# mLSTM with both parts summed in PSUM from scaled queries, and 24 modulation vectors of layer 0 on the matrix engine

## The chip, the cores and the metric

The kernel runs on one core of a Trainium2 chip. The metric is the device time of one execution in microseconds (us), here the median of three runs. PE is the matrix engine, DVE the vector engine, ACT the scalar engine, POOL the GpSimd engine, SP the queue that issues the loads and stores.

## What is computed

One inference step of two layers over 1152 tokens (1024 latent tokens and 128 context tokens) of width 1024. Each layer modulates its input with six vectors of 1024 made from `c` (latent tokens) and `c_ctx` (context tokens), projects it to three groups of heads (latent attention, mLSTM, HGRN2), joins them by an output projection, and ends in a gated feed-forward part. What the change touches is the modulation and the mLSTM:

```python
mod = (jax.nn.silu(cvec) @ lp['w_mod'] + lp['b_mod'])[:, None, :]
sh1, sc1, g1, sh2, sc2, g2 = jnp.split(mod, 6, axis=-1)
...
def step(carry, inp):                      # mlstm_scan, one chunk, one direction
    ...
    mt = jnp.maximum(a, Dm.max(-1))
    ws = jnp.exp(a - mt)
    qk = jnp.einsum('bhtd,bhsd->bhts', qc, kc) * jnp.exp(Dm - mt[..., None])
    num = ws[..., None] * jnp.einsum('bhtd,bhde->bhte', qc, C) + jnp.einsum('bhts,bhse->bhte', qk, vc)
    den = ws * jnp.einsum('bhtd,bhd->bht', qc, n) + qk.sum(-1)
    h = num / jnp.maximum(jnp.abs(den), jnp.exp(-mt))[..., None]
...
h = hf + flip(hb)                          # mlstm_mixer: both directions, then per head
mu = h.mean(-1, keepdims=True)
var = jnp.mean(jnp.square(h - mu), -1, keepdims=True)
h = (h - mu) * lax.rsqrt(var + EPS)
```

## The kernel before

The two layers run one after the other, each in four phases: A (all input projections, HGRN2, the preparation of attention, mLSTM), B (attention), C (output projection, layer norm), D (feed-forward). Instructions are not left in the order of the source: a list scheduler places each on its engine as soon as its inputs and its buffers allow, the one that stands first in the source going first. Each engine then runs its own list strictly in order, and SP issues nearly all loads and stores, also in order. Matmuls with an accurate product are written as three (L155, L156, L157: high by high, low by high, high by low part); those of the mLSTM are plain float32.

**Modulation.** The 48 vectors of a layer's `w_mod`, 128 results each, are 512 KB apiece. At the very start of the kernel vectors 8 to 15 of layer 0 are made on PE (L251 in `start`, eight matmuls of 128x2 each) and vectors 0 to 7 on DVE. The other vectors of layer 0 up to 39 are made by `start_mod` on DVE, where `mod_gemv` does two products with a sum over 1024 columns per vector (L213), each with a read of the accumulator, and `mod_bias` adds the bias (L220) for eight vectors at once. Vectors 16 to 23 run beside the `gi` projection and the preparation of attention in phase A; behind them a small transposition on PE (`gsave`, L225) writes them out. Vectors 24 to 39 run in the mLSTM loop of layer 0, two after each chunk. Layer 1's vectors are made elsewhere and are not touched.

**mLSTM.** `mlstm` is called at the end of phase A of each layer and runs over nine chunks of 128 tokens; the ninth holds the context tokens and has no earlier state. Per chunk, SP loads a stabiliser table `nb` (broadcast, 512 KB) and the queries `qc`. PE makes the four query-key products (L832); POOL masks (L834), ACT takes eight exponentials of 128x128 (L837), DVE multiplies the two (L841, four times 256 columns). Then, for each direction, PE makes the part from the state (L847, two matmuls of 130 columns) in one PSUM bank; DVE scales it by `ws` into SBUF (L848); PE makes the part inside the chunk (L852, four matmuls of 65 columns) in another bank; DVE adds it (L855, or L857 in the ninth chunk). Denominators are three small operations on DVE (L860, L861, L862). The division (L865, twice) runs on POOL in layer 0 and on DVE in layer 1, POOL adds the directions (L866), DVE takes mean and variance (L869, L871, L873), POOL the power (L874), and two passes subtract the mean and scale (L876, on POOL in layer 0, on DVE in layer 1). The exponentials `ws` are made earlier, in `ml_gates`.

Behind the loop in the source stand two spills (`mo`, `gg`: projections with 256 columns in the banks of the ring `r_mm`, three of the eight PSUM banks), and then phase B. The scheduler pulls matmuls of both into the mLSTM's stretch. The first attention scores are L1136, with a row maximum on DVE (L1137) between them; L1182 is the first use of the finished weights.

## Time and profile before

| what | us |
|---|---|
| median of 3 runs | 3642.04 (3641.22 to 3644.99) |
| the profiled execution | 3641.28 |
| its span in the trace | 3639.5 |
| PE busy | 3405.9 |
| DVE busy | 2264.8 |
| layer 0, first L832 to first L1182 (479.6 to 613.7) | 134.1 |
| layer 1, the same (2288.1 to 2393.7) | 105.6 |

The profile gives one execution; every duration comes from it. A busy PE is counted by records, whose ends are modelled; the clock granted to PE is given for a stretch as a share of the full 2.4 GHz, 0.50 being 1.2 GHz. A wait is the idle time of an engine just before an instruction, with the one that released it.

### The profile page before, as it was taken

How to read it: one execution, taken by the hardware profiler on the slowest of the kernel's cores; microseconds unless marked ns; L12 is line 12 of the kernel's file. 1: busy time of each engine (PE TensorE's matmuls, PEld its weight loads, DVE VectorE, ACT ScalarE, POOL GpSimd, SP SyncE). 2: the span in 40 equal slices, each digit the busy share in tenths (PEclk: the TensorE clock that was granted, in tenths of full speed). 3: DMA queues.
4: the chain of work that ended last, by engine and by line, in shares of the span. 5: the costliest groups of instructions: out<-in, count | busy, mean ns of one | idle time of the engine just before them, and what ended most of it. 6: DMA issues, size and time to landing. Idle time of an engine off the chain costs nothing. (4 is left out here: it accounts for less than half of the span.)

```text
span 3639.5 us, 56085 instructions
## 1 busy us (share of the span) xinstructions
PE 3405.9 (94%) x20556; PEld 3034.6 (83%) x20556; DVE 2264.8 (62%) x4492; ACT 1635.7 (45%) x2877; POOL 1988.8 (55%) x1745
## 2 busy tenths in 40 slices
PE   7999987999989999999889989989999999999997
PEld 7998875776779999988689888877767899998875
DVE  6868878555674444487775678765558544443246
ACT  4264564887343333312272636577853433333211
POOL 3455566777665555401453556567863555552176
PEclk9899976999989999999999999789999999999998
DMA  6212153002352222375422021401044322224222
GB/s 244 72 40 43 39 167 100 18 21 81 121 160 85 85 85 85 111 252 179 156 79 62 30 45 34 137 25 25 22 132 139 110 73 73 73 74 139 94 99 80
DMA packets 331272, 335.77 MB, mean 92 GB/s; under 512 B 191458, under 2 KB 270386, under 8 KB 330996
## 3 DMA queue, kind: packets, MB, share of 16 engines
q1 hardware_dynamic: 330996, 332.19, 29.5%
q8 instruction: 161, 2.64, 0.3%
q14 instruction: 115, 0.94, 0.1%
HBM read 263.54 MB, written 68.56 MB: 91 GB/s over the span
## 5 line engine op out<-in xcount | busy, mean ns | idle before, releaser
L151 POOL TENSOR_TENSOR t<-t,t 128x512 fp32r<-128x512 f32 (+3 forms) x318 | 437.8, 1378 | 374.8 <-ACT t L150 374.4
L150 ACT CAST t<-t 128x512 fp32r<-128x512 f32 (+5 forms) x404 | 270.7, 673 | 698.0 <-PE bank L1449 278.7
L1449 PE MATMUL bank<-hhi,t 128*128 128x256 f32 (+1 forms) x2816 | 570.8, 295 | 12.4 <-DVE t L1349 11.5
L155 PE MATMUL bank<-hhi,t 128*128 128x384 f32 (+1 forms) x1220 | 455.1, 378 | 19.2 <-ACT t L150 5.1
L157 PE MATMUL bank<-hhi,t 128*128 128x384 f32 (+1 forms) x1220 | 460.0, 378 | 8.8 <-DVE t L151 8.8
L1449 PEld LDWEIGHTS bank<-hhi,t 128*128 128x128 f32 x2816 | 456.2, 189 | 13.6 <-ACT t L150 12.3
L156 PE MATMUL bank<-hlo,t 128*128 128x384 f32 (+1 forms) x1220 | 460.9, 378 | 4.9 <-POOL hlo L151 4.1
L1187 POOL TENSOR_TENSOR t<-t,t 128x512 fp32r<-128x512 f32 (+1 forms) x304 | 383.3, 1281 | 125.4 <-ACT t L1186 103.0
L1449 PE MATMUL bank<-t,t 128*128 128x320 f32 (+1 forms) x3168 | 434.2, 297 | 2.3 <-DVE t L1507 1.7
L1449 PEld LDWEIGHTS bank<-t,t 128*128 128x128 f32 x3168 | 427.9, 190 | 3.7 <-DVE t L1507 1.9
L1449 PE MATMUL bank<-hlo,t 128*128 128x320 f32 (+1 forms) x1408 | 415.2, 295 | 0.0
L155 PE MATMUL bank<-t,hhi 128*128 128x256 f32 (+3 forms) x1232 | 386.8, 315 | 12.1 <-DVE t L1107 5.4
L156 PE MATMUL bank<-t,hhi 128*128 128x256 f32 (+3 forms) x1232 | 388.0, 315 | 4.3 <-POOL t L146 4.3
L157 PE MATMUL bank<-t,hlo 128*128 128x256 f32 (+3 forms) x1232 | 388.4, 316 | 0.3 <-POOL hlo L151 0.3
L155 PEld LDWEIGHTS bank<-hhi,t 128*128 128x128 f32 x1220 | 237.9, 196 | 57.3 <-ACT t L150 6.7
L1137 DVE TENSOR_REDUCE t<-bank 128x1 f32<-128x384 f32 (+1 forms) x400 | 203.9, 538 | 122.6 <-PE bank L1136 119.5
L157 PEld LDWEIGHTS bank<-hhi,t 128*128 128x128 f32 x1220 | 240.1, 197 | 39.2 <-DVE t L151 12.1
L156 PEld LDWEIGHTS bank<-hlo,t 128*128 128x128 f32 x1220 | 239.6, 196 | 34.7 <-POOL hlo L151 5.1
L1449 PEld LDWEIGHTS bank<-hlo,t 128*128 128x128 f32 x1408 | 265.4, 188 | 0.3 <-issue 0.2
L155 PEld LDWEIGHTS bank<-t,hhi 128*128 128x128 f32 x1232 | 239.8, 195 | 30.2 <-DVE t L1107 5.6
L213 DVE SCALAR_TENSOR_TENSOR t<-t,t 128x1024 bf16<-128x1024 f32 x176 | 239.3, 1359 | 40.6 <-DMA t<-in_w_mod_dram 31.6
L156 PEld LDWEIGHTS bank<-t,hhi 128*128 128x128 f32 x1232 | 240.4, 195 | 20.1 <-POOL t L146 4.7
(355 smaller groups left out, 7329.1 us busy)
## 6 DMA issues: line engine op xcount, KB each, us to landing
t<-in_w_mod_dram SPq DMA_DIRECT2D x96, 512.0 KB
t<-in_w_ffn_in_dram SPq DMA_DIRECT2D x88, 512.0 KB
t<-in_w_ffn_out_dram SPq DMA_DIRECT2D x44, 512.0 KB
t<-in_w_in_dram SPq DMA_DIRECT2D x40, 512.0 KB
shid<-t SPq DMA_DIRECT2D x88, 160.0 KB
sx<-t SPq DMA_DIRECT2D x27, 512.0 KB
t<-sx SPq DMA_DIRECT2D x27, 512.0 KB
shid<-t SPq DMA_DIRECT2D x88, 128.0 KB
```

Of the source, the lines that this page charges most:

```text
L150: self.nc.scalar.copy(hi, src)
L151: (eng or self.nc.gpsimd).tensor_tensor(lo, src, hi.bitcast(F32), op=ALU.subtract)
L155: mm(ps, a[0], b[0], start=first, stop=False)
L156: mm(ps, a[0], b[1], start=False, stop=False)
L157: mm(ps, a[1], b[0], start=False, stop=last)
L213: nc.vector.scalar_tensor_tensor(junk, raw, 1.0, cB[s], op0=ALU.mult, op1=ALU.mult, accum_out=self.modfm[:, l, j, s:s + 1])
L1137: V.tensor_reduce(nm[:, i, b:b + 1] if i < 8 else nm[:, i, 3:4], ps, axis=AX.X, op=ALU.max, negate=True)
L1187: G.tensor_tensor(pl, e, ph.bitcast(F32), op=ALU.subtract)
L1449: mm(ps, a[x][:, k * P:(k + 1) * P], view(y, k, n0, n1), start=first and k == 0 and i == 0, stop=k == 3 and i == 2, skip_group_check=True)
```

## The change

In the mLSTM, the scale `ws` goes to the queries instead of to the product: SP loads the exponents broadcast over partitions (two loads per chunk and eight chunks per layer), ACT takes one Exp of 128x512, POOL multiplies by the queries, and PE's state part (now L862) and inside part (L865) accumulate in one PSUM bank per direction. L848, L855 and L857 are gone. The four products of L841 become two of 512 columns (L856). Denominators and the division (L869 to L875) read PSUM on DVE, in both layers. The last subtraction and scaling become four ACT operations of 128x64 per chunk (L888), with one small operation on DVE for the bias (L886).

The 24 vectors 16 to 39 of layer 0 are made on PE (L292, eight matmuls of 128x2 each, from a transposed packing of `w_mod`), three after each chunk of layer 0's mLSTM, into a PSUM bank of their own. That bank is taken from `r_mm`, which has two banks for the spills there. The preparation of attention has no vectors beside it any more, and `gsave` of vectors 16 to 23 moves into the mLSTM. Three buffers of 512 KB take turns for the loads, where there were two.

```diff
-    def start_mod(self, z, j0, j1):
-        raw = z.ring(2, [P, U])
-        cB, junk = [z([P, D]), z([P, D])], z([P, D], BF16)
-        self.mod_init(cB)
+    def start_mod(self, z, j0, j1, bank):
+        nc = self.nc
+        raw = z.ring(3, [P, U])
 
         def gen():
             for j in range(j0, j1):
-                self.mod_gemv(0, j, cB, raw.next(), junk)
+                w, ps = raw.next(), bank[:, 2 * (j - j0):2 * (j - j0) + 2]
+                nc.sync.dma_start(w, self.ins["w_mod"][0, j])
+                for i in range(KD):
+                    nc.tensor.matmul(ps, w[:, i * P:(i + 1) * P], self.cc[:, i, :], start=(i == 0), stop=(i == KD - 1))
                 if j % 8 == 7:
-                    self.mod_bias(0, j - 7, 8)
+                    g = j - 7
+                    b = self.col(0, "bmod")[:, g:g + 8].unsqueeze(2).to_broadcast([P, 8, 2])
+                    pv = bank[:, 2 * (g - j0):2 * (g - j0) + 16].rearrange("p (j s) -> p j s", s=2)
+                    nc.vector.scalar_tensor_tensor(self.modfm[:, 0, g:g + 8, :], pv, 1.0 if (g // 8) % 3 == 1 else 0.0, b,
+                                                   op0=ALU.add, op1=ALU.add)
...
-                        bg = self.start_mod(Zone(self, c, "gemv"), 16, 24) if l == 0 else iter(())
+                        bg = iter(())
...
-                bg = self.start_mod(zl, 24, 40) if l == 0 else iter(())
+                bg = iter(())
+                if l == 0:
+                    self.r_mm = self.banks(0, 1)
+                    bg = self.start_mod(zl, 16, 40, self.bank[2])
...
-            nc.scalar.activation(ws[:, :, 4 * d:4 * d + 4], nts[:, :, 2 + d, :], AF.Exp)
...
+            if n < 8:
+                wq = rwq.next()
+                for e in range(2):
+                    nc.sync.dma_start(wq[64 * e:64 * e + 64], bass.AP(tensor=sws.tensor, offset=sws.offset + e * T + n * P,
+                                                                      ap=[[0, 64], [4 * T, 2], [2 * T, 2], [1, P]]))
+                nc.scalar.activation(wq, wq, AF.Exp)
+                G.tensor_tensor(wq, wq, qc.unsqueeze(1).to_broadcast([P, 2, 2, P]), op=ALU.mult)
...
-                for d in range(2):
-                    V.tensor_tensor(nbv[:, d, :, e, :], psq[e][:, 0:256].rearrange("p (a t) -> p a t", a=2), nbv[:, d, :, e, :], op=ALU.mult)
-            num = rnum.next()
+                pq = psq[e][:, 0:256].rearrange("p (a t) -> p a t", a=2).unsqueeze(1).to_broadcast([P, 2, 2, P])
+                V.tensor_tensor(nbv[:, :, :, e, :], pq, nbv[:, :, :, e, :], op=ALU.mult)
+            den, pv = rden.next(), []
             for d in range(2):
+                ps = self.r_m.next()
                 if n < 8:
-                    psn = self.r_m.next()
                     for p in range(2):
-                        nc.tensor.matmul(psn[:, p * 130:(p + 1) * 130], qc[:, p, :], Cst[d][:, n, p].rearrange("p e c -> p (e c)"), start=True, stop=True)
-                    V.tensor_tensor(num[:, d], psn[:, 0:260].rearrange("p (h c) -> p h c", h=4),
-                                    ws[:, n, 4 * d:4 * d + 4].unsqueeze(2).to_broadcast([P, 4, 65]), op=ALU.mult)
-                psi = self.r_m.next()
+                        nc.tensor.matmul(ps[:, p * 130:(p + 1) * 130], wq[:, d, p, :], Cst[d][:, n, p].rearrange("p e c -> p (e c)"),
+                                         start=(p == 0), stop=False, skip_group_check=True)
                 for h in range(4):
-                    nc.tensor.matmul(psi[:, h * 65:(h + 1) * 65], nb[:, 4 * d + h, :], vaug[:, n, h, :], start=True, stop=True)
-                pv = psi[:, 0:260].rearrange("p (h c) -> p h c", h=4)
-                if n < 8:
-                    V.tensor_tensor(num[:, d], pv, num[:, d], op=ALU.add)
-                else:
-                    V.tensor_copy(num[:, d], pv)
-            den = rden.next()
-            dv = den.rearrange("p (d h) -> p d h", d=2)
-            V.scalar_tensor_tensor(dv, num[:, :, :, 64], -1.0, num[:, :, :, 64], op0=ALU.mult, op1=ALU.max)
-            V.tensor_tensor(den, den, emt[:, n, :], op=ALU.max)
-            V.reciprocal(den, den)
-            h1 = rh.next()
+                    nc.tensor.matmul(ps[:, h * 65:(h + 1) * 65], nb[:, 4 * d + h, :], vaug[:, n, h, :], start=(n == 8 and h == 0),
+                                     stop=(h == 3), skip_group_check=True)
+                pv.append(ps[:, 0:260].rearrange("p (h c) -> p h c", h=4))
+                dd = den[:, 4 * d:4 * d + 4]
+                V.tensor_tensor(dd, pv[d][:, :, 64], emt[:, n, 4 * d:4 * d + 4], op=ALU.max)
+                V.scalar_tensor_tensor(dd, pv[d][:, :, 64], -1.0, dd, op0=ALU.mult, op1=ALU.max)
+            rd = den[:, 0:8]
+            V.reciprocal(rd, rd)
+            hs = [rh.next() for _ in range(2)]
             for d in range(2):
-                (LG).tensor_tensor(num[:, d, :, 0:64], num[:, d, :, 0:64], den[:, 4 * d:4 * d + 4].unsqueeze(2).to_broadcast([P, 4, 64]), op=ALU.mult)
-            G.tensor_tensor(h1, num[:, 0, :, 0:64], num[:, 1, :, 0:64], op=ALU.add)
+                V.tensor_tensor(hs[d], pv[d][:, :, 0:64], den[:, 4 * d:4 * d + 4].unsqueeze(2).to_broadcast([P, 4, 64]), op=ALU.mult)
+            h1 = hs[0]
+            G.tensor_tensor(h1, h1, hs[1], op=ALU.add)
...
-            for i, op in ((0, ALU.subtract), (1, ALU.mult)):
-                (LG).tensor_tensor(h1, h1, mv[:, :, i:i + 1].to_broadcast([P, 4, 64]), op=op)
+            V.scalar_tensor_tensor(mb, mv[:, :, 0], -1.0, rs, op0=ALU.mult, op1=ALU.mult)
+            for h in range(4):
+                nc.scalar.activation(h1[:, h, :], h1[:, h, :], AF.Identity, bias=mb[:, h:h + 1], scale=mv[:, h, 1:2])
...
-            for _ in range(2):
+            for _ in range(3):
```

How the work stands on PE in the middle of layer 0's mLSTM, before. L832 are query-key products, L847 state parts, L852 inside parts; L155 to L157 belong to a spill:

```order
L832 MATMUL bank_66<-t_4391,t_612 128x128 x2
L157 MATMUL bank_63<-t_131,hlo_77 128x256
L155 MATMUL bank_63<-t_131,hhi_76 128x256
L156 MATMUL bank_63<-t_135,hhi_76 128x256
L157 MATMUL bank_63<-t_131,hlo_77 128x256
L847 MATMUL bank_69<-t_2979,t_4387 128x130 x2
L847 MATMUL bank_68<-t_2983,t_4387 128x130
L852 MATMUL bank_70<-t_608,t_4371 128x65 x3
L847 MATMUL bank_68<-t_2983,t_4387 128x130
L832 MATMUL bank_67<-t_4391,t_612 128x128 x2
L155 MATMUL bank_64<-t_147,hhi_76 128x256
```

Between the mLSTM's matmuls stand runs of 256-column matmuls; no vector is on PE. After, at about the same chunk (L847 is now the query-key product, L862 the state part, L865 the inside part, L292 a vector, `x8` its eight matmuls, `bank_65` the vectors' bank):

```order
L292 MATMUL bank_65<-cc_84,t_4284 128x2
L292 MATMUL bank_65<-cc_84,t_4288 128x2 x8
L292 MATMUL bank_65<-cc_84,t_4292 128x2 x8
L847 MATMUL bank_66<-t_4320,t_608 128x128
L847 MATMUL bank_67<-t_4320,t_608 128x128
L847 MATMUL bank_66<-t_4320,t_608 128x128
L847 MATMUL bank_67<-t_4320,t_608 128x128
L862 MATMUL bank_69<-t_2918,t_4332 128x130 x2
L862 MATMUL bank_70<-t_2922,t_4332 128x130 x2
L292 MATMUL bank_65<-cc_84,t_4284 128x2 x7
L865 MATMUL bank_69<-t_604,t_4300 128x65 x4
L865 MATMUL bank_70<-t_604,t_4300 128x65 x4
```

Vectors, three per chunk, stand between the inside parts of one chunk and the products of the next, and again ahead of the inside parts; in this place there is no matmul of a spill. The first vector stands behind most of the spills' matmuls and the last some 110 rows later; between them are nine matmuls of 256 and six of 384 columns.

On DVE, in the middle of layer 0's mLSTM, before (L151 splits operands of attention):

```order
L848 TENSOR_TENSOR t_4399<-bank_69,t_2807 128x260
L151 TENSOR_TENSOR hlo_77<-t_5692,hhi_76 128x384 x2
L213 SCALAR_TENSOR_TENSOR t_4361,modfm_80<-t_4349,t_4357 128x1024
L151 TENSOR_TENSOR hlo_77<-t_5692,hhi_76 128x384
L855 TENSOR_TENSOR t_4395<-bank_68,t_4395 128x260
L862 RECIPROCAL t_4407<-t_4407 128x8
L873 TENSOR_SCALAR t_4439<-t_4439 128x4
L855 TENSOR_TENSOR t_4399<-bank_70,t_4399 128x260
L213 SCALAR_TENSOR_TENSOR t_4361,modfm_80<-t_4345,t_4353 128x1024
L860 SCALAR_TENSOR_TENSOR t_4411<-t_4395 128x8
L841 TENSOR_TENSOR t_4375<-bank_66,t_4375 128x2x128 x2
```

After, at the same chunk's place:

```order
L856 TENSOR_TENSOR t_4300<-bank_66,t_4300 128x4x128
L856 TENSOR_TENSOR t_4300<-bank_67,t_4300 128x4x128
L869 TENSOR_TENSOR t_4340<-bank_69,t_2744 128x4
L870 SCALAR_TENSOR_TENSOR t_4340<-bank_69,t_4340 128x4
L869 TENSOR_TENSOR t_4340<-bank_70,t_2744 128x4
L870 SCALAR_TENSOR_TENSOR t_4340<-bank_70,t_4340 128x4
L297 SCALAR_TENSOR_TENSOR modfm_80<-bank_65,cols_78 128x16
L872 RECIPROCAL t_4340<-t_4340 128x8
L875 TENSOR_TENSOR t_4352<-bank_69,t_4340 128x256
L875 TENSOR_TENSOR t_4356<-bank_70,t_4340 128x256
```

The L213 are gone from between the mLSTM's operations, and one L297 per eight vectors adds the bias out of the vectors' bank.

On PE in phase A, before, inside the input projections of 176 columns:

```order
L157 MATMUL bank_64<-t_131,hlo_77 128x176
L155 MATMUL bank_64<-t_131,hhi_76 128x176
L156 MATMUL bank_64<-t_135,hhi_76 128x176
L225 MATMUL bank_68<-ident_71,modfm_80 16x128
L157 MATMUL bank_64<-t_131,hlo_77 128x176
L155 MATMUL bank_65<-t_147,hhi_76 128x176
```

After, the same transposition (now L226) stands in layer 0's mLSTM, behind the first eight vectors:

```order
L862 MATMUL bank_68<-t_2918,t_4324 128x130 x2
L862 MATMUL bank_69<-t_2922,t_4324 128x130 x2
L156 MATMUL bank_64<-t_136,hhi_76 128x256
L157 MATMUL bank_64<-t_132,hlo_77 128x256
L226 MATMUL bank_70<-ident_71,modfm_80 16x128
L292 MATMUL bank_65<-cc_84,t_4292 128x2 x8
L865 MATMUL bank_68<-t_604,t_4308 128x65 x4
```

It moved out of the projections of phase A.

## Rows read from the trace of the kernel before

**Rows 1.** The page, part 1: busy us (share of the span) and count per engine.

```profile
PE 3405.9 (94%) x20556; PEld 3034.6 (83%) x20556; DVE 2264.8 (62%) x4492; ACT 1635.7 (45%) x2877; POOL 1988.8 (55%) x1745
```

**Rows 2.** Windows: us, busy by engine (count), PE clock, DMA share, GB/s.

```profile
479.60:613.70 134.10, 96.33 (x464) 81.07 (x464) 119.84 (x325) 54.82 (x121) 94.86 (x96) 0.68 0.50 157
2288.10:2377.70 89.60, 78.62 (x420) 71.44 (x419) 74.72 (x261) 53.04 (x131) 52.28 (x61) 0.72 0.47 138
2288.10:2393.70 105.60, 88.00 (x443) 77.59 (x443) 89.11 (x286) 59.00 (x140) 55.10 (x65) 0.68 0.41 123
```

**Rows 3.** Lines of DVE, 479.6 to 613.7: busy us, mean ns, idle before, releaser.

```profile
L213 DVE SCALAR_TENSOR_TENSOR t<-t,t 128x1024 bf16<-128x1024 f32 x32 | 44.1, 1377 | 5.7 <-DMA t<-in_w_mod_dram 3.7 <-DMA t<-scr 1.9
...
L213 DVE DVE_READ_ACCUMULATOR t<-t,t 128x1 f32 x32 | 2.5, 77 | 0.0
```

**Rows 4.** Window of phase A, layer 0.

```profile
80.00:140.00 60.00, 49.13 (x349) 47.56 (x348) 59.97 (x122) 23.88 (x31) 31.27 (x26) 0.85 0.29 94
```

**Rows 5.** Lines of DVE, 70 to 140.

```profile
L213 DVE SCALAR_TENSOR_TENSOR t<-t,t 128x1024 bf16<-128x1024 f32 x16 | 20.9, 1309 | 4.6 <-DMA t<-scr 4.6
```

**Rows 6.** Waits of PE, 70 to 150: line, releaser, us, times, longest.

```profile
PE bank L225 <- DVE modfm L220: 4.2, 1, 4.2
```

**Rows 7.** Timeline of PE: start us, us, line, tiles, form, count.

```profile
24.07 3.41 PE L251 MATMUL bank<-t,t 128*128 128x2 f32 x16
27.34 0.67 PE L155 MATMUL bank<-hhi,t 128*128 128x384 f32 x1
...
34.72 1.84 PE L251 MATMUL bank<-t,t 128*128 128x2 f32 x16
36.42 0.42 PE L155 MATMUL bank<-hhi,t 128*128 128x384 f32 x1
```

**Rows 8.** Windows that show the granted clock.

```profile
34.00:37.00 3.00, 3.00 (x25) 3.00 (x24) 0.37 (x3) 0.08 (x1) 1.80 (x1) 1.00 1.02 405
51.00:56.00 5.00, 5.00 (x18) 5.00 (x19) 3.72 (x10) 2.17 (x2) 0.00 (x0) 0.50 0.01 3
510.00:520.00 10.00, 5.76 (x24) 5.05 (x23) 9.94 (x29) 7.45 (x18) 5.93 (x6) 0.50 0.82 260
2310.00:2330.00 20.00, 20.00 (x97) 18.63 (x98) 16.38 (x58) 16.42 (x52) 8.22 (x11) 0.50 0.51 154
2350.00:2360.00 10.00, 9.10 (x67) 8.59 (x67) 10.00 (x45) 2.89 (x5) 6.63 (x9) 1.00 0.30 95
```

**Rows 9.** Lines of PE, 2310 to 2330.

```profile
L852 PE MATMUL bank<-t,t 128*128 128x65 f32 x46 | 10.7, 411 | 0.0
L847 PE MATMUL bank<-t,t 128*128 128x130 f32 x24 | 6.8, 448 | 0.0
L832 PE MATMUL bank<-t,t 64*128 64x128 f32 x26 | 4.7, 461 | 0.0
```

**Rows 10.** Lines of DVE, 2288.1 to 2393.7 (layer 1's mLSTM).

```profile
L841 DVE TENSOR_TENSOR t<-bank,t 128x256 f32<-128x256 f32 x36 | 14.0, 411 | 7.5 <-ACT t L837 6.1 <-PE bank L832 0.7 <-issue 0.6
L876 DVE TENSOR_TENSOR t<-t,t 128x256 f32<-128x256 f32 x18 | 9.8, 551 | 0.1
...
L855 DVE TENSOR_TENSOR t<-bank,t 128x260 f32<-128x260 f32 x16 | 6.6, 412 | 0.1
L848 DVE TENSOR_TENSOR t<-bank,t 128x260 f32<-128x260 f32 x16 | 6.5, 416 | 5.1 <-PE bank L847 5.1
...
L860 DVE SCALAR_TENSOR_TENSOR t<-t 128x8 f32<-128x8 f32 x9 | 3.5, 391 | 0.0
```

**Rows 11.** Waits of PE, 2288.1 to 2393.7.

```profile
PE bank L1136 <- DVE t L1137: 6.4, 3, 3.4
...
PE bank L852 <- DVE t L841: 1.8, 2, 1.1
```

**Rows 12.** Lines of ACT, 2288.1 to 2393.7.

```profile
L837 ACT ACTIVATE t<-t,t 128x128 f32<-128x128 f32 x72 | 21.8, 387 | 1.8 <-POOL t L834 1.7
```

**Rows 13.** The page, part 5: a costly group of POOL.

```profile
L1187 POOL TENSOR_TENSOR t<-t,t 128x512 fp32r<-128x512 f32 (+1 forms) x304 | 383.3, 1281 | 125.4 <-ACT t L1186 103.0
```

More of the change, by code (lines that the diff above doesn't have):

```diff
@@ L175, in setup @@
         self.mhalf = t(self.pp, [P, 8], name="mhalf")
+        self.cc = t(self.pp, [P, KD, 2], name="cc")
         nc.vector.memset(self.mhalf, -0.5)
@@ L237, in start @@
         accs = [(i // NB, i % NB, self.bank[i]) for i in range(7)]
-        cin, cc = z([P, KD, 2]), z([P, KD, 2])
+        cin, cc = z([P, KD, 2]), self.cc
         cB, junk = [z([P, D]), z([P, D])], z([P, D], BF16)
@@ L814, in mlstm @@
         at, emt, ws, uw, sc = gates
-        snr = self.s_nr
-        LG = V if l else G
+        snr, sws = self.s_nr, self.s_ws
         rNB = pool.ring(4, [P, 8, P])
         rq = pool.ring(3, [P, 2, P])
-        rnum = pool.ring(3, [P, 2, 4, 65])
-        rden = pool.ring(2, [P, 8])
-        rh = pool.ring(3, [P, 4, 64])
+        rwq = pool.ring(3, [P, 2, 2, P])
+        rden = pool.ring(2, [P, 12])
+        rh = pool.ring(4, [P, 4, 64])
         rst = pool.ring(2, [P, 4, 6])
@@ L871, in mlstm @@
                 V.bn_aggr(mv[:, h, :], st[:, h, :])
-            rs = mv[:, :, 1]
+            rs, mb = mv[:, :, 1], den[:, 8:12]
             V.tensor_scalar(rs, rs, EPS, None, op0=ALU.add)
             G.tensor_tensor(rs, rs, mhalf, op=ALU.pow)
-            for i, op in ((0, ALU.subtract), (1, ALU.mult)):
-                (LG).tensor_tensor(h1, h1, mv[:, :, i:i + 1].to_broadcast([P, 4, 64]), op=op)
+            V.scalar_tensor_tensor(mb, mv[:, :, 0], -1.0, rs, op0=ALU.mult, op1=ALU.mult)
+            for h in range(4):
+                nc.scalar.activation(h1[:, h, :], h1[:, h, :], AF.Identity, bias=mb[:, h:h + 1], scale=mv[:, h, 1:2])
             nc.sync.dma_start(self.s_rec[n * P:(n + 1) * P, 0:256], h1.rearrange("p h c -> p (h c)"))
-            for _ in range(2):
+            for _ in range(3):
                 next(bg, None)
@@ L1701, in pack @@
         wm[0, :, :, :8].transpose(2, 3, 0, 1).reshape(8, P, 1024),
-        wm[0, :, :, 8:16].transpose(2, 1, 0, 3).reshape(8, P, 1024),
-        wm[0, :, :, 16:].transpose(2, 3, 0, 1).reshape(32, P, 1024),
+        wm[0, :, :, 8:40].transpose(2, 1, 0, 3).reshape(32, P, 1024),
+        wm[0, :, :, 40:].transpose(2, 3, 0, 1).reshape(8, P, 1024),
         wm[1].transpose(2, 3, 0, 1).reshape(48, P, 1024)], 0).reshape(DEPTH, 48, P, 1024)
```

## The prediction

> **What bounds the kernel now.** I read the totals of the page first: PE is busy 3405.9 us of a span of 3639.5 us, DVE 2264.8 [rows 1]. PE is the engine that counts, so a change is worth what it does to PE's idle time, to PE's own work and to PE's clock. Then I cut out the two stretches that run the code in question, from the first L832 of a layer's mLSTM to the first L1182 of its attention, and read one row each [rows 2]. Layer 0: 134.1 us, PE busy 96.33, DVE 119.84, clock 0.68. Layer 1: 105.6 us, PE busy 88.00, DVE 89.11, clock 0.68. The two differ by 28.5 us, and the work that only layer 0 has there is the GEMV of 16 vectors: 32 L213 of 1377 ns and their reads, 44.1 + 2.5 = 46.6 us of DVE [rows 3]. So in layer 0 this stretch waits for DVE, which had 46.6 us more and gave 28.5 of them to the clock on the wall. In layer 1 PE is busy 83% of the stretch, so there PE itself is already most of the bound. The third place is phase A of layer 0: over 80 to 140 us DVE is busy 59.97 of 60 us, PE 49.13 [rows 4]; the GEMV of eight vectors sits there on DVE [rows 5]. Outside these three places the change touches nothing. PE is nearly full after them, so what they gain or lose I carry to the end undiminished.
>
> **The vectors on PE: the term that decides.** A vector is now eight matmuls 128x2 (L292), each with a weight load of 128 columns. The trace has the same form at the start of the kernel, L251, and two pairs of rows bracket its price [rows 7]: sixteen records (two for a float32 matmul) start at 34.72 and the next matmul starts at 36.42, which is 1.70 us; another sixteen start at 24.07 and the next matmul at 27.34, which is 3.27 us. The pairs differ by the clock: the first stands among dense 384-column matmuls at a granted clock of 1.00, the second is twice as long, as at 0.50. For 24 vectors that is 40.8 us at the fast level (2.4 GHz) and 78.5 at the slow one (1.2 GHz). Nothing of it lies beside other PE work, since PE runs in order; only PE's idle time can swallow it.
>
> The Trainium skill ("TensorE: Matmul & The Clock Gate", Part 2, "Back-to-back issue gap") gives about 81 ns for a sustained pair of weight load and 128-column matmul; an estimate from that page is 16 x 0.081 = 1.3 us a vector and 31 us for 24, below both rows; the rows decide, and the page's figure is left out of the sum.
>
> Which level? A full PE doesn't settle it: from 51 to 56 us PE is busy 5.00 of 5.00 us at 0.50, and in 2310 to 2330 it is busy all 20 us at 0.50, while 2350 to 2360, busy 9.10 of 10, has 1.00 [rows 8]. What runs in 2310 to 2330 are the mLSTM's narrow matmuls, 46 L852, 24 L847 and 26 L832 [rows 9]. The order of the changed kernel decides which of these its stretch will resemble: of the spills' 256-column matmuls nine stand among the vectors, the others ahead of the first; between the first vector and the last, 24 vectors and the mLSTM matmuls of eight chunks alternate, with six of 384 columns. That is like 2310 to 2330, only with narrower matmuls yet. I take 3.27 us for all 24: **+78.5 us** of PE work.
>
> **Layer 0's stretch.** The base is layer 1's stretch, the same code without a GEMV: 105.6 us. From it I take the 6 us that the new mLSTM gives (next part), 99.6. The vectors add 78.5. They fill PE's idle time before the attention: layer 1 has 89.6 - 78.62 = 11.0 us up to its first L1136 [rows 2], much of it inside short waits where no vector is at hand; I take 6. So 99.6 + 78.5 - 6 = 172.1, against 134.1: **+38 us**. The ends: at 1.70 us a vector and an unchanged clock for the rest, 99.6 + 40.8 - 6 = 134.4, no change; with layer 1's 78.62 busy us also brought from its mean clock of 0.72 to 1.00, 22 us less, **-22**; with all at the slow level and the vectors' loads on time, some 10 us more than forecast, **+48**. DVE is then no longer near the bound: of its 119.84 us 46.6 go, and what the rewritten mLSTM takes off and puts on (in layer 0 also the division, so far on POOL) about cancels, some 73 us in 172.
>
> **The mLSTM rewritten, priced in layer 1.** DVE loses L848 and L855 (6.5 + 6.6 us), two passes of L876 (9.8), and half of the instructions of L841 (36 of 411 ns become 18 of twice the width: between 7.4 and 14.8 us, I take 12, so 2 off) [rows 10]. For nine small L860 and nine L861 it gets 36 small operations out of PSUM, and nine for the normalisation: 27 more, at half to all of L860's 391 ns [rows 10] 5 to 11 us. The division stays on DVE. That is 6.5 + 6.6 + 9.8 + 2 - 8 = about 17 us off 89.11. But PE had been waiting little for this: of its 17.6 us of idle time, 6.4 is L1136 behind L1137, at the end of the stretch, where DVE is still catching up, and the mLSTM's waits for DVE are 1.8 and smaller [rows 11]. The work of PE itself is unchanged: as many matmul records, each inter part merely accumulates into the bank of the intra part. So the gain is bounded by DVE's backlog at L1136 and the small waits: I take **-6 us**, ends -12 and +3.
>
> The new side chain costs PE little. Per chunk two more loads of 128 KB, one Exp of 128x512 on ACT (between the 387 ns of a 128x128 Exp, L837, and four times that [rows 12]) and one product 128x512 on POOL (L1187: 1281 ns [rows 13]); in layer 0 POOL loses the divisions and the normalisation. ACT has 59.00 of 105.6 us taken [rows 2]; four small normalisations, at most 0.39 us each, and the Exp add some 2.5 us a chunk, 22 in all, which fit. The scaled queries depend on nothing of the chunk before, so they run ahead by the ring of three; if they didn't in one chunk, PE would stand for a load, an Exp and a product, some 3 us: that is the +3 end.
>
> **Phase A of layer 0.** Eight vectors leave DVE there: 16 L213 of 1309 ns, 20.9 us [rows 5], out of 60 busy us [rows 4]. PE idles 60 - 49.13 = 10.9 us. Directly seen: a transposition (L225) that waits 4.2 us on PE for the bias behind those vectors goes away with them [rows 6]; of the other 6.7 us of idle time I give half, and nothing for the clock. **-8 us**, ends 0 and -15. Two banks instead of three for the 256-column spills cost nothing visible: while one bank is drained the next fills over 24 matmuls.
>
> **Sum.** 3641.3 (the profiled execution; its span is 3639.5) + 38 - 6 - 8 = 3665.3. The median of the runs is 0.8 above the profiled one: **3666 us**.
>
> **Rivals.**
> A, faster: the clock stays up. PE has no more gaps in layer 0's stretch, and the slow level there comes from the gaps that DVE tore (0.50 in 510 to 520, with PE busy 5.76 of 10 us [rows 8]). Then vectors cost 1.70, the mLSTM's matmuls run at 1.00 too, and the stretch is 112: 3641.3 - 22 - 6 - 8 + 0.8 = 3606. Against it speaks 2310 to 2330 [rows 8]. The point from which it decides: the change comes out even at a price of some 2.3 us a vector (99.6 + 55 - 6 = 148.6, +14.5, eaten by the -14 elsewhere), a mean clock about that of layer 1's stretch, 0.72; above it the kernel gains.
> The Trainium skill (same page, "Loop structure matters more than you think") says that matmuls kept back to back stay at the fast level, and by that rule A would happen. This trace disagrees with it in 2310 to 2330 [rows 8], where PE without a gap stays at 0.50 for 20 us; that is why A gets no more than its chance below.
>
> B, even: vectors at a mixed price near 2.3 us, since some of them meet the large matmuls that the order leaves among them. Time 3635 to 3649.
>
> C, slower still: PE now stands in line behind the weight loads. A vector on PE waits for its 512 KB, and behind it on PE stand the mLSTM's matmuls. On SP the loads stand in one queue with the chunks' loads, and each waits until its slot of three is read. At 405 GB/s (34 to 37 us [rows 8]) a load takes 1.3 us, so 24 exposed loads would be 31 us; I put half: 3681. For it speaks the stretch's traffic, 157 GB/s [rows 2], against it the ring of three and PE's slow pace per vector. It decides if PE's waits in the stretch name w_mod.
>
> **How the numbers follow.** Forecast (slow level, PE the bound) 0.58, with its own range 3650 to 3682; C 0.10, to 3690; B 0.12; A 0.20, spread over 3606 to 3634. About 0.2% (7 us) is what a measurement of this kernel can tell from no change: faster 0.20, same 0.12, slower 0.68. A range that leaves out no more than 2 in 10 takes in half of A: 3624 to 3690.
>
> **What would show it.** The stretch of layer 0: 172 us, clock 0.5 to 0.6 while L292 runs, sixteen records taking about 3.3 us, PE busy over 90%, DVE under half. Layer 1's stretch: about 100 us, L1136's wait for L1137 shorter, no L876 on DVE. Phase A: 80 to 140 us with fewer gaps on PE, no wait of the transposition there. I am wrong if the clock in the vectors' stretch is above 0.72 (A), if PE waits for w_mod by more than 10 us in all (C), or if phase A gives over 15.

## The result, and the profile after

The changed kernel takes 3677.35 us (median of 4 runs, 3672.99 to 3685.93) beside 3641.63 us of the kernel before; the ratio is 1.0100, 95% interval 1.0083 to 1.0117. It is slower by 1.0%, some 36 us. The profiled execution has a span of 3672.8 us, 33.3 more than before.

The page, part 1, of the changed kernel (busy us, share of the span, count), which answers to [rows 1]:

```profile
PE 3473.9 (95%) x20940; PEld 3117.5 (85%) x20940; DVE 2174.5 (59%) x4346; ACT 1675.0 (46%) x2965; POOL 1955.8 (53%) x1725
```

DVE has 90 us less, PE 68 us more. Windows of the changed kernel (start and end; us; busy us with count of PE, of its weight loads PEld, of DVE, ACT and POOL; PE clock, DMA share, GB/s): layer 0's stretch from the first query-key product to the first use of the weights, 120 us out of it, layer 1's stretch, and phase A; they answer to [rows 2, 4, 8]:

```profile
460.70:644.40 183.70, 169.70 (x828) 161.28 (x827) 78.19 (x257) 76.98 (x179) 60.48 (x70) 0.59 0.46 148
480.00:600.00 120.00, 120.00 (x575) 118.15 (x575) 41.49 (x161) 40.49 (x105) 35.64 (x44) 0.50 0.51 165
2324.80:2430.90 106.10, 91.15 (x446) 79.98 (x446) 68.89 (x245) 74.59 (x181) 61.00 (x71) 0.68 0.44 134
80.00:140.00 60.00, 58.36 (x498) 57.44 (x498) 42.29 (x155) 21.76 (x34) 29.87 (x31) 1.00 0.18 50
```

Layer 0's stretch is 183.7 us instead of 134.1. For 120 us on end PE has no gap at all, at a clock of 0.50. DVE, 119.84 us busy before, has 78.19. Layer 1's stretch is 106.1 instead of 105.6, although DVE lost 20 us there (89.11 to 68.89). Phase A gained: over 80 to 140 us PE is busy 58.36 instead of 49.13 us at 1.00 instead of 0.85, and layer 0's stretch begins at 460.7 instead of 479.6.

Lines of PE in layer 0's stretch (line, tiles, form, count, busy us, mean ns, idle before, releaser), and two rows of its timeline (start us, us):

```profile
L292 PE MATMUL bank<-cc,t 128*128 128x2 f32 x384 | 80.2, 342 | 0.0
...
L862 PE MATMUL bank<-t,t 128*128 128x130 f32 x64 | 17.8, 450 | 5.4 <-POOL t L843 5.4
```

```profile
545.62 7.35 PE L292 MATMUL bank<-cc,t 128*128 128x2 f32 x34
552.90 1.23 PE L847 MATMUL bank<-t,t 64*128 64x128 f32 x8
```

34 records of vectors start at 545.62 and the next matmul at 552.90: 0.214 us a record, 3.43 us a vector of sixteen. That is the slow one of the two prices in [rows 7]. No wait in the stretch names the loads of `w_mod`.

The ledger of the profiled executions, by the starts of the two stretches and the spans: phase A and what is ahead of it -18.9 us, layer 0's stretch +49.6, the rest of layer 0 up to layer 1's stretch +6.0, that stretch +0.5, the remainder -3.9; sum +33.3. The +6.0 and -3.9 lie where the change moves nothing, and aren't explained.

### The profile page after: what moved, and what is told of

Read it like the earlier page. It is cut to its first block, busy times and chain, and to the rows that moved or that the text cites. A ratio compares the mean times of both kernels' runs of the same rounds, so it can differ in the third digit from the quotient of the medians.

```text
span 3672.8 us, 56819 instructions
## 1 busy us (share of the span) xinstructions
PE 3473.9 (95%) x20940; PEld 3117.5 (85%) x20940; DVE 2174.5 (59%) x4346; ACT 1675.0 (46%) x2965; POOL 1955.8 (53%) x1725
## 5 line engine op out<-in xcount | busy, mean ns | idle before, releaser
L151 POOL TENSOR_TENSOR t<-t,t 128x512 fp32r<-128x512 f32 (+3 forms) x318 | 437.0, 1376 | 384.9 <-ACT t L150 384.1
L155 PE MATMUL bank<-hhi,t 128*128 128x384 f32 (+1 forms) x1220 | 450.8, 375 | 11.8 <-ACT t L150 5.0
L157 PE MATMUL bank<-hhi,t 128*128 128x384 f32 (+1 forms) x1220 | 453.6, 373 | 7.4 <-DVE t L151 7.4
L156 PE MATMUL bank<-hlo,t 128*128 128x384 f32 (+1 forms) x1220 | 452.7, 372 | 3.7 <-POOL hlo L151 3.7
L155 PE MATMUL bank<-t,hhi 128*128 128x256 f32 (+3 forms) x1232 | 385.3, 314 | 7.5 <-ACT t L509 2.0
L157 PE MATMUL bank<-t,hlo 128*128 128x256 f32 (+3 forms) x1232 | 385.8, 314 | 0.0
L1149 DVE TENSOR_REDUCE t<-bank 128x1 f32<-128x384 f32 (+1 forms) x400 | 204.7, 540 | 122.6 <-PE bank L1148 119.7
L155 PEld LDWEIGHTS bank<-hhi,t 128*128 128x128 f32 x1220 | 235.9, 194 | 44.6 <-ACT t L150 6.1
L157 PEld LDWEIGHTS bank<-hhi,t 128*128 128x128 f32 x1220 | 235.5, 193 | 37.6 <-DVE t L151 10.9
L155 PEld LDWEIGHTS bank<-t,hhi 128*128 128x128 f32 x1232 | 237.6, 193 | 27.0 <-ACT t L509 2.2
L157 PEld LDWEIGHTS bank<-t,hlo 128*128 128x128 f32 x1232 | 238.6, 194 | 14.9
```

The lines of the kernel that those rows point to most:

```text
L151: (eng or self.nc.gpsimd).tensor_tensor(lo, src, hi.bitcast(F32), op=ALU.subtract)
L155: mm(ps, a[0], b[0], start=first, stop=False)
L156: mm(ps, a[0], b[1], start=False, stop=False)
L157: mm(ps, a[1], b[0], start=False, stop=last)
L1149: V.tensor_reduce(nm[:, i, b:b + 1] if i < 8 else nm[:, i, 3:4], ps, axis=AX.X, op=ALU.max, negate=True)
```

## The experiments

All ratios are against the kernel before, measured beside each. "Stretch" is the one of layer 0 as above, in the profiled execution.

| kernel | mLSTM | vectors 16 to 39 of layer 0 | median us | ratio (95%) | stretch us |
|---|---|---|---|---|---|
| before | old | DVE | 3641.63 | 1 | 134.1 |
| changed | new | PE, 128x2, in mLSTM | 3677.35 | 1.0100 (1.0083 to 1.0117) | 183.7 |
| mlstm_only | new | DVE | 3646.59 | 1.0015 (1.0001 to 1.0029) | 139.0 |
| gemv_only | old | PE, 128x2, in mLSTM | 3674.02 | 1.0077 (1.0051 to 1.0104) | 189.6 |
| no_vectors | new | left out | 3636.08 | 0.9972 (0.9958 to 0.9985) | 116.4 |
| vectors_twice | new | PE, 128x2, twice | 3771.92 | 1.0346 (1.0318 to 1.0373) | 275.0 |
| vec_dense | new | PE, 128x2, in phase A | 3684.59 | 1.0116 (1.0094 to 1.0137) | 112.8 |
| vec_moving | new | PE, 2x128, in mLSTM | 3640.94 | 0.9996 (0.9983 to 1.0008) | 131.4 |
| dense_moving | new | PE, 2x128, in phase A | 3642.02 | 1.0002 (0.9991 to 1.0013) | 103.3 |
| norm_back | new, normalised as before | PE, 2x128, in mLSTM | 3645.51 | 1.0013 (1.0000 to 1.0026) | 134.0 |
| mixed8 | old | 16 on DVE, 8 on PE, 128x2 | 3631.16 | 0.9973 (0.9962 to 0.9984) | 143.4 |
| old_ml_moving8 | old | 16 on DVE, 8 on PE, 2x128 | 3630.45 | 0.9976 (0.9965 to 0.9988) | 134.9 |
| old_ml_moving24 | old | PE, 2x128, in mLSTM | 3616.12 | 0.9938 (0.9920 to 0.9955) | 123.6 |
| new_ml_layer1 | old in layer 0, new in layer 1 | as the row above | 3631.94 | 0.9962 (0.9948 to 0.9976) | 122.7 |

### One part at a time: mlstm_only and gemv_only

mlstm_only is the kernel before with the function `mlstm` of the changed one, and its two vectors per chunk on DVE (the main line, against the changed kernel):

```diff
-            for _ in range(3):
+            for _ in range(2):
                 next(bg, None)
```

> The kernel before with the new mLSTM alone: the 24 vectors stay on DVE, eight in phase A and sixteen in layer 0's mLSTM. Theory (PE's vectors at the slow level are the loss, the rewritten mLSTM is about neutral): 3634 to 3642 us, layer 1's stretch about 106 us, layer 0's 128 to 134 us. Rival (the rewritten mLSTM loses by its longer chain over SP, ACT and POOL): 3650 us or more, both stretches longer than before.

gemv_only is the changed kernel with the old function `mlstm` put back, three vectors per chunk, and the exponentials `ws` that it needs (the first line against the changed kernel, the others against the old function):

```diff
+            nc.scalar.activation(ws[:, :, 4 * d:4 * d + 4], nts[:, :, 2 + d, :], AF.Exp)
...
-            for _ in range(2):
+            for _ in range(3):
                 next(bg, None)
```

> The changed kernel with the old mLSTM in both layers: only the 24 vectors move to PE. Theory: within 8 us of the changed kernel, 3669 to 3685 us, with the clock at 0.50 while the vectors run. Rival (the mLSTM's rewriting loses): near the kernel before, 3640 to 3650 us.

Measured: 3646.59 and 3674.02 us. So the loss is the vectors' on PE, as the theory had it. mlstm_only lies above its range, between it and the rival's 3650; its layer 0 stretch, 139.0, is longer than expected too. Beside a kernel before of 3642.96 it is 0.15% slower, with an interval that just excludes no change. Windows of mlstm_only's stretch and of gemv_only's, with 120 us out of it, and PE's waits in mlstm_only (line, releaser, us, times, longest):

```profile
478.50:617.50 139.00, 93.33 (x464) 83.42 (x463) 110.46 (x313) 71.83 (x165) 70.58 (x68) 0.63 0.56 167
```

```profile
460.00:649.60 189.60, 173.22 (x838) 164.38 (x838) 81.50 (x267) 61.46 (x137) 73.89 (x98) 0.57 0.42 133
480.00:600.00 120.00, 117.34 (x562) 115.44 (x562) 43.48 (x166) 28.90 (x72) 45.29 (x67) 0.50 0.43 138
```

```profile
PE bank L852 <- DVE t L865: 24.0, 6, 5.4
PE bank L837 <- DVE t L846: 6.9, 2, 5.3
```

The old mLSTM with vectors on PE has the same 0.50 over 480 to 600. In mlstm_only PE stands 24.0 us in front of L852, the state part, until L865, the division, has read a PSUM bank: the new mLSTM frees its banks only after the division, and that stands in DVE's row behind the GEMV (the vectors there). DVE has 9.4 us less than before (110.46 instead of 119.84), PE's idle time is 7.9 us longer (45.7 instead of 37.8). That this wait eats the relief is the reading of these rows; no run frees the banks earlier.

### The price of a vector: no_vectors and vectors_twice

```diff
-                nc.sync.dma_start(w, self.ins["w_mod"][0, j])
-                for i in range(KD):
-                    nc.tensor.matmul(ps, w[:, i * P:(i + 1) * P], self.cc[:, i, :], start=(i == 0), stop=(i == KD - 1))
+                if j == j0:
+                    nc.vector.memset(bank[:, 0:64], 0.0)
```

> The changed kernel without the 24 vectors: their loads and matmuls are left out, the bank that they would fill is set to zero. Theory (they cost PE 24 x 3.3 us and almost nothing hides it): layer 0's stretch falls from 183.7 to 100 to 110 us, the total to 3595 to 3605 us. Rival (PE would have idled half of it anyway, behind DVE, ACT or loads): stretch 140 us, total 3635 us.

```diff
-                for i in range(KD):
+                for i in [*range(KD)] * 2:
```

> The changed kernel with each vector's eight matmuls issued twice from the same loaded weights, so 192 more matmuls and no more traffic. Theory (PE bound at the slow level): plus 24 x 3.3 = 78 us, 3755 us, clock 0.50 over the whole stretch. Rivals: the clock rises once PE is fuller, plus 41 us (3718 us); or loads bound the stretch, plus under 20 us.

Measured: stretches of 116.4 and 275.0 us, medians 3636.08 and 3771.92. Windows of no_vectors' stretch, its longest wait of PE, and windows of vectors_twice:

```profile
457.80:574.20 116.40, 83.52 (x453) 74.00 (x452) 71.32 (x250) 77.11 (x179) 60.70 (x70) 0.74 0.43 125
```

```profile
PE bank L864 <- DVE t L855: 13.7, 1, 13.7
```

```profile
458.30:733.30 275.00, 252.47 (x1214) 244.30 (x1213) 73.69 (x252) 76.43 (x178) 60.68 (x70) 0.56 0.33 99
480.00:660.00 180.00, 179.94 (x873) 178.11 (x873) 31.48 (x140) 26.79 (x81) 25.76 (x32) 0.51 0.31 95
```

The second set of vectors costs PE 252.47 - 169.70 = 82.8 us of work and the stretch 275.0 - 183.7 = 91.3 us. The first adds 169.70 - 83.52 = 86.2 us of work and only 183.7 - 116.4 = 67.3 to the stretch: 18.9 us fall into idle time, of which the stretch without vectors has 32.9 us and the one with them 14.0 (13.7 of the 32.9 are one wait near its start, for the product L855 that follows ACT's exponentials). So the price per vector and the bound by PE are shown. The total of vectors_twice lies 17 us above its expected 3755.

The total of no_vectors missed the middle of its range by 36 us and came out at the rival's 3635, though not for the rival's reason: the stretch was 116.4 and not 140 (nor 100 to 110). Its profiled execution lost some 20 us again from layer 1's stretch on, where its instructions are those of the changed kernel; 16 of them lie behind that stretch, with a clock of 0.96 instead of 0.99 in the first 320 us there. Why isn't known (the modulation that it leaves out also changes the numbers that later layers compute with); by medians the vectors cost 41 us, by the stretch 67.

### What keeps the clock low: vec_dense, vec_moving, dense_moving

The prediction had put the slow level down to a stretch of narrow matmuls; by that reading a vector among wide ones costs 1.70 us. vec_dense moves them there:

```diff
+                        if l == 0:
+                            self.r_mm = self.banks(0, 1)
+                            bg = self.start_mod(Zone(self, c, "gemv"), 16, 40, self.bank[2])
...
-                            next(bg, None)
+                            for _ in range(3):
+                                next(bg, None)
```

> The changed kernel with its 24 vectors moved: three of them after each token tile of the gi projection in phase A of layer 0, among dense 256-column matmuls, instead of in the mLSTM. Theory (the slow level is that of a stretch made of narrow matmuls; among dense ones a vector costs 1.7 us): clock near 1.0 in 80 to 160 us, phase A 24 x 1.7 = 41 us longer than in the changed kernel, layer 0's mLSTM stretch 116 us, total 3650 us. Rival (the vectors pull the clock down wherever they stand): phase A 70 us longer or more, clock 0.5 there, total 3680 us.

Measured: 3684.59 us, with phase A 73 us longer than in the changed kernel (layer 0's stretch begins at 534.1 instead of 460.7); the theory fell, and the rival's 70 us and 3680 came out. A window of phase A and its timeline around two vectors:

```profile
100.00:180.00 80.00, 80.00 (x447) 79.94 (x446) 3.35 (x10) 1.82 (x3) 4.95 (x7) 0.61 0.32 106
```

```profile
103.84 0.28 PE L156 MATMUL bank<-t,hhi 128*128 128x256 f32 x1
103.96 0.28 PE L157 MATMUL bank<-t,hlo 128*128 128x256 f32 x1
104.08 4.20 PE L292 MATMUL bank<-cc,t 128*128 128x2 f32 x32
108.14 0.56 PE L155 MATMUL bank<-t,hhi 128*128 128x256 f32 x1
108.50 0.41 PE L156 MATMUL bank<-t,hhi 128*128 128x256 f32 x1
108.71 0.41 PE L157 MATMUL bank<-t,hlo 128*128 128x256 f32 x1
```

The 256-column matmuls ahead of the vectors start 0.12 us apart, those behind them 0.21: 32 records of vectors stand between. Over 80 us with PE full the clock is 0.61. The vectors cost their neighbours the clock too. The row from which the 1.70 us came, a lone vector among 384-column matmuls at a clock of 1.00 [rows 7, 8], was no measure for three of them at every 24 matmuls.

vec_moving exchanges the operands. The two columns of `c` are now the stationary side (the operand of the weight load), and the weight block is the moving side (the operand of the matmul itself); the result comes as two rows and is turned by small transpositions:

```diff
-                    nc.tensor.matmul(ps, w[:, i * P:(i + 1) * P], self.cc[:, i, :], start=(i == 0), stop=(i == KD - 1))
+                    nc.tensor.matmul(bank[0:2, i0 * P:(i0 + 1) * P], self.cc[:, i, :], w[:, i * P:(i + 1) * P], start=(i == 0), stop=(i == KD - 1))
...
+                    row = rows.next()
+                    nc.vector.tensor_copy(row, bank[0:2, 0:3 * P])
...
+                nc.tensor.transpose(bank[:, 384 + 2 * (j - j0):386 + 2 * (j - j0)], row[0:2, i * P:(i + 1) * P], self.ident[0:2, 0:2])
```

> The changed kernel with the operands of each vector's matmuls exchanged: the two columns of c are the stationary side and the 128x128 weight block moves, so a weight load has 2 columns instead of 128 and a matmul 128 instead of 2; 24 small transpositions and 8 copies are added. Theory (a record of the vectors costs what the load of 128 stationary columns costs, 0.2 us at the slow level): under 2 us a vector, layer 0's stretch 130 to 150 us, total 3640 to 3655 us. Rival (the price is that of a record, whichever side moves): 3.3 us a vector, stretch and total as in the changed kernel, 3677 us, or longer by the transpositions.

Measured: 3640.94 us, stretch 131.4. Windows, timeline and the wait for loads (L306 is the vectors' line):

```profile
467.70:599.10 131.40, 118.22 (x849) 95.02 (x849) 75.73 (x248) 70.60 (x166) 60.79 (x69) 0.90 0.67 206
500.00:560.00 60.00, 58.88 (x498) 46.98 (x497) 38.01 (x138) 26.42 (x75) 26.71 (x34) 1.00 0.80 248
```

```profile
520.07 1.91 PE L306 MATMUL bank<-t,cc 128*2 128x128 f32 x16
521.91 1.16 PE L876 MATMUL bank<-t,t 128*128 128x130 f32 x8
...
526.95 5.40 PE L306 MATMUL bank<-t,cc 128*2 128x128 f32 x48
532.28 0.71 PE L876 MATMUL bank<-t,t 128*128 128x130 f32 x4
```

```profile
PE bank L306 <- DMA t<-in_w_mod_dram: 4.1, 2, 3.5
```

The number came out as expected, the reason didn't. Sixteen records take 1.84 us (520.07 to 521.91), 48 take 5.33 (526.95 to 532.28), so 1.78 to 1.84 us a vector. The 128x2 form takes 1.70 at 1.00 [rows 7]. A record costs about the same whichever side has the 128 columns; what changed is the clock, 1.00 over 500 to 560, with the mLSTM's own narrow matmuls still there. dense_moving is vec_dense with the same exchange in its `start_mod`:

> As vec_dense (24 vectors among the 256-column matmuls of phase A) with the weight block as the moving side. Theory (two moving columns bring the clock down also for their neighbours, 128 don't): clock 0.95 to 1.00 in 80 to 180 us where vec_dense had 0.61, phase A 43 us longer than without vectors, total 3645 to 3655 us. Rival (vectors anywhere cost the clock): total as vec_dense, 3685 us.

Measured: 3642.02 us, 3 below its range, against 3684.59 of vec_dense with the operands the other way round. The window that had 0.61:

```profile
100.00:180.00 80.00, 80.00 (x698) 70.61 (x697) 22.64 (x112) 4.91 (x12) 13.21 (x16) 1.00 0.42 132
```

So in phase A it is the form with two moving columns that brings the clock down: without vectors its neighbours have 1.00 (80 to 140 us of the changed kernel), and beside 128 moving columns of the same float32 matmul they keep it. In the mLSTM the vectors are not the only thing that goes with the slow level. In layer 1 of vec_moving, where no vector stands, PE is at 0.50 over 50 us with the mLSTM's products and few others, as in 2310 to 2330 before [rows 8]; in layer 0, with vectors of 128 moving columns among them, the same products have 1.00 and take 276 ns instead of 408. The window of layer 1, and lines of PE in it and in 500 to 560:

```profile
2295.00:2345.00 50.00, 47.76 (x206) 43.76 (x205) 32.19 (x130) 35.28 (x97) 30.18 (x36) 0.50 0.43 132
```

```profile
L879 PE MATMUL bank<-t,t 128*128 128x65 f32 x96 | 22.6, 408 | 0.5 <-DVE t L870 0.5
```

```profile
L306 PE MATMUL bank<-t,cc 128*2 128x128 f32 x277 | 32.3, 272 | 0.0
L879 PE MATMUL bank<-t,t 128*128 128x65 f32 x96 | 12.8, 276 | 0.1
```

So there the exchanged vectors go with a higher clock than the products have alone. What in a matmul's form decides it, no run shows.

### Fewer vectors on PE: mixed8 and old_ml_moving8

Both keep the old mLSTM, and vectors 24 to 39 on DVE in it; only 16 to 23 leave phase A for PE, in the form of the change (mixed8) or with the operands exchanged (old_ml_moving8).

```diff
-                bg = self.start_mod(zl, 24, 40) if l == 0 else iter(())
+                    bp, bd = self.start_pe(zl, 16, 24, self.bank[2]), self.start_mod(zl, 24, 40)
```

> The kernel before (old mLSTM, vectors 24 to 39 on DVE in it) with only vectors 16 to 23 changed: made on PE in layer 0's mLSTM, one per chunk, not on DVE in phase A. Theory (phase A's gain of 15 us is that of DVE without these eight, and PE's idle time of 38 us in layer 0's stretch hides part of 8 x 3.3 = 26 us): phase A 15 us shorter, the stretch 5 to 15 us longer, total 3632 to 3640 us. Rival (the vectors' price is not hidden because PE stands where DVE makes it wait): stretch 26 us longer or more, 3653 us.

> As mixed8 (old mLSTM, vectors 24 to 39 on DVE, 16 to 23 on PE), with the weight block as the moving side for those eight. Theory (clock): 3618 to 3629 us, below mixed8, with a granted clock above mixed8's 0.63 in the stretch. Rival (DVE with its sixteen vectors bounds the stretch whatever PE's clock): as mixed8, 3631 us.

Measured: 3631.16 and 3630.45 us, both faster than before and not to be told apart. Windows of the two stretches, and PE's longest waits in the second:

```profile
457.00:600.40 143.40, 122.05 (x582) 110.22 (x582) 113.39 (x324) 55.33 (x134) 87.96 (x99) 0.62 0.56 178
```

```profile
462.10:597.00 134.90, 99.05 (x590) 80.89 (x589) 119.16 (x330) 62.56 (x144) 93.69 (x101) 0.77 0.59 192
```

```profile
PE bank L155 <- ACT t L150: 12.6, 1, 12.6
PE bank L155 <- DVE t L1157: 10.6, 3, 6.9
```

For mixed8 the theory holds, with a total just below its range: the stretch begins some 22 us earlier (457.0 instead of 479.6; 15 were expected), and is 9 us longer. For old_ml_moving8 the rival holds in its total: the clock rose from 0.62 to 0.77, PE's busy time fell by 23 us, and the stretch by 8.5; with sixteen vectors DVE is busy 119.16 us, and PE waits for ACT and DVE at the attention's first projections.

### The version that beats both: old_ml_moving24, and what the rewriting costs

old_ml_moving24 is gemv_only with the `start_mod` of vec_moving: the old mLSTM, and all 24 vectors on PE with the operands exchanged.

> The old mLSTM in both layers, all 24 vectors on PE in layer 0's mLSTM with the weight block as the moving side. Theory (the loss was the clock that vectors of two moving columns bring down; at 1.00 a vector costs 1.8 us and DVE is free): clock near 1.0 in layer 0's stretch, its length 115 to 130 us, phase A 15 us shorter, total 3615 to 3630 us, faster than both kernels. Rival (the old mLSTM, with its waits of PE for DVE between its two parts, leaves PE's gains unused): stretch 140 us or more, total 3640 us or more.

Measured: 3616.12 us, 0.62% below the kernel before (interval 0.45 to 0.80%) and 61 us below the changed one.

```profile
464.00:587.60 123.60, 115.58 (x837) 93.11 (x835) 80.24 (x264) 54.54 (x123) 70.84 (x96) 0.90 0.63 202
500.00:560.00 60.00, 60.00 (x503) 49.15 (x501) 35.43 (x136) 12.23 (x36) 36.53 (x58) 1.00 0.66 209
```

With all vectors off DVE and the clock at 1.00 over 500 to 560 (0.90 over the stretch), the stretch is 123.6 us with PE busy 115.58. Against vec_moving, 3640.94, it differs only by the mLSTM: by the two ratios (0.9996 and 0.9938) the rewriting now costs some 21 us. (Beside vectors of the slow form it made no difference that can be told: the changed kernel's 1.0100 and gemv_only's 1.0077 have overlapping intervals.) Two runs look for the 21 us. norm_back undoes its last part in vec_moving:

```diff
-            V.scalar_tensor_tensor(mb, mv[:, :, 0], -1.0, rs, op0=ALU.mult, op1=ALU.mult)
-            for h in range(4):
-                nc.scalar.activation(h1[:, h, :], h1[:, h, :], AF.Identity, bias=mb[:, h:h + 1], scale=mv[:, h, 1:2])
+            for i, op in ((0, ALU.subtract), (1, ALU.mult)):
+                (V if l else G).tensor_tensor(h1, h1, mv[:, :, i:i + 1].to_broadcast([P, 4, 64]), op=op)
```

> As vec_moving with one part of the mLSTM's rewriting undone: subtracting the mean and scaling return from ACT to two passes of 256 columns (on POOL in layer 0, on DVE in layer 1). Theory (in layer 1 the time that DVE saved went into waits behind ACT, whose queue got the normalisation and the Exp of the scales): layer 1's stretch 2 to 6 us below vec_moving's 109, total 3633 to 3640 us. Rival (ACT's share is hidden): no difference beyond 3 us, 3641 us.

Measured: 3645.51 us, not faster. Layer 1's stretch of norm_back:

```profile
2292.70:2402.40 109.70, 88.44 (x445) 77.90 (x444) 78.51 (x253) 62.44 (x145) 62.02 (x71) 0.72 0.43 130
```

109.7 us, as vec_moving's 109.1: taking the four normalisations off ACT and back to DVE doesn't shorten it. new_ml_layer1 puts the rewritten mLSTM into layer 1 of old_ml_moving24:

```diff
-                self.mlstm(l, gates, vaug, mkT, Cst, zl, bg)
+                (self.mlstm_new if l else self.mlstm)(l, gates, vaug, mkT, Cst, zl, bg)
```

> As old_ml_moving24, the fastest so far at 3616 us, with the rewritten mLSTM in layer 1 alone, where no vectors stand. It measures the rewriting by itself. The prediction's theory (DVE's relief is worth 6 us): 3610 us. Theory now (DVE's relief goes into waits behind ACT and PE's own slow level, and the stretch was 0 to 5 us longer in the other kernels): 3616 to 3624 us, stretch 104 to 110. Rival (the rewriting makes most of the 25 us between vec_moving, 3641, and old_ml_moving24, and does so in layer 1): 3630 us or more.

Measured: 3631.94 us beside a kernel before of 3644.19. The ratio is 0.9962 beside old_ml_moving24's 0.9938, so it is some 9 us slower by the ratios, with intervals that overlap. The total lies above the theory's 3616 to 3624, at the rival's 3630, but layer 1's stretch isn't where it is lost. Layer 1's stretch and 30 us of the attention behind it, of new_ml_layer1 and then of old_ml_moving24:

```profile
2266.00:2370.00 104.00, 88.74 (x448) 77.52 (x447) 73.06 (x247) 74.50 (x181) 61.55 (x71) 0.70 0.46 137
2400.00:2430.00 30.00, 28.25 (x123) 22.09 (x122) 14.43 (x28) 21.78 (x41) 19.16 (x15) 0.83 0.06 11
```

```profile
2265.40:2370.00 104.60, 85.62 (x444) 75.13 (x442) 89.02 (x284) 58.82 (x140) 55.40 (x65) 0.72 0.42 123
2400.00:2430.00 30.00, 29.86 (x154) 23.39 (x153) 16.68 (x33) 26.20 (x52) 24.59 (x20) 1.00 0.06 11
```

The stretch is as long as with the old mLSTM, 104.0 and 104.6 us. The loss in the profiled execution comes behind it: in 2400 to 2430 the clock is 0.83 instead of 1.00, and from the end of the stretch to the end of the kernel it takes 1260.9 us instead of 1244.8. The rewriting doesn't bring that by itself: no edit touches the code there, and with the rewritten mLSTM in layer 1 this time is 1241.5 us in dense_moving, 1241.8 in the changed kernel and 1257.9 in no_vectors, with the old one 1244.8 to 1249.2 in five kernels. What does bring it isn't known. Between the profiled executions of vec_moving and old_ml_moving24 lie 25 us: some 4 ahead of layer 0's stretch, 8 in it (131.4 beside 123.6 us), 5 in layer 1's and 8 behind it. So 12 of them lie in the two stretches that run the rewritten code.

## Why the prediction was right

It forecast 3666 us and slower, for the reason that PE becomes the bound of layer 0's stretch at the slow level. The direction and that reason hold; the size lay within the range because terms that were off partly cancelled.

- **The vectors' price.** 3.27 us was taken, 3.43 measured; 78.5 us forecast, 82.8 by doubling. The choice of the slow end was right. The reason given for it was half right: PE full at 0.50 in 2310 to 2330 did show that a full PE doesn't suffice, and the mLSTM's products do have the slow level by themselves. But the neighbours don't settle a vector's price: vectors of two moving columns were slow among wide matmuls too (0.61 in vec_dense), and with 128 moving columns the mLSTM's products ran at 1.00.
- **Layer 0's stretch, +38 forecast, +49.6 measured, 2 above its upper end.** The mis-sized term is the base. 99.6 us was taken from layer 1's stretch; without vectors layer 0's is 116.4, with 13.7 us in one wait near its start. The other two terms were off against each other: PE's work rose by 86.2 us and not 78.5 (some 82 for the vectors, by estimate from 3.43 each, the rest other matmuls at a lower clock), and 18.9 us of idle time were filled and not 6. 116.4 + 86.2 - 18.9 is 183.7.
- **Layer 1, -6 forecast, +0.5 measured.** The wait of L1136 behind L1137 did shorten, 6.4 us [rows 11] to 1.4 in the row below (now L1148 behind L1149), but the wait for the product with the exponentials grew from 1.8 us [rows 11] to 3.4 (now L865 behind L856), and a new one of 2.9 stands in front of the state part L862, for the bank that the division L875 holds:

```profile
PE bank L865 <- DVE t L856: 3.4, 3, 2.4
PE bank L862 <- DVE t L875: 2.9, 1, 2.9
...
PE bank L1148 <- DVE t L1149: 1.4, 2, 1.2
```

  In all, PE's idle time fell only from 17.6 to 15.0 us, and its busy time rose from 88.00 to 91.15. The step that failed is that less work on DVE would shorten PE's waits by as much: the banks that the new mLSTM holds until the division weren't priced.
- **Phase A, -8 forecast, -18.9 measured, beyond its end of -15.** The prediction itself had named more than 15 us as a sign that it is wrong. Waits were given half, the clock nothing. PE's idle time over 80 to 140 fell from 10.9 to 1.6 us and the clock rose from 0.85 to 1.00. The start of the stretch was at 457.0 to 469 us in every kernel that took the eight vectors out of phase A and left nothing in their place, and at 479 in mlstm_only, which left them.
- **The sum**: +24 forecast, +49.6 - 18.9 + 0.5 = +31 by the same terms. Layer 0's stretch and layer 1's were 18 us too low together and phase A 11 too high; that they partly cancel is luck.
- **The rivals.** A fell as it was put: PE had no gap for 120 us, and the clock stayed at 0.50. The Trainium skill's rule ("TensorE: Matmul & The Clock Gate", "Loop structure matters more than you think"), by which back-to-back matmuls stay fast, is not borne out by this stretch. An estimate from the Trainium skill's 81 ns a pair (same page, "Back-to-back issue gap") is 1.3 us a vector, where the rows at 1.00 show 1.70 to 1.84. What A would have brought was there all the same: with the operands exchanged the clock stayed up, which gave nothing over the kernel before with the new mLSTM (0.9996) and some 23 us (0.62%) with the old one. B's mixed price didn't come about: 3.43 us is the slow one. C didn't happen in the changed kernel; at the faster price, 4.1 us of waits for `w_mod` appear in vec_moving.

## What to carry to other kernels

A busy engine isn't a fast one: before moving small products to the matrix engine, look at the granted clock of rows with the same form, and try the form with the operands exchanged, since here it cost about the same per record and the clock stayed up. Take work off the vector engine where it stands at 100% beside a matrix engine that waits (phase A gave 19 us for eight vectors), but price what then comes last, PSUM banks that are held longer among it. When a change bundles two edits, time them apart: the vectors were worth some 23 us in another form, and the rewriting gained nothing in any pair of runs.

## What the runs showed of the hardware

A float32 matmul of 128x128 by 2 columns and one of 128x2 by 128 columns cost about the same per record at a clock of 1.00, 0.106 and 0.111 to 0.115 us. PE without a gap ran at 0.50 for 120 us where 319 of its 575 records were of the first form, between narrow products of the mLSTM. Such products ran at 0.50 over 50 us (PE busy 47.8) without any vector, too, and at 1.00 over 60 us where 277 of 498 records were of the second form. 256-column matmuls 0.12 us apart came 0.21 us apart behind two vectors of the first form, at 0.61 over 80 us; with the second form there, PE, full again, had 1.00 over the same 80 us.
